# Weight sums made by DMAs that add onto the loaded operand: two of four sums moved, loads six steps ahead

## The chip, the cores and the metric

The kernel runs on one core of a Trainium2 chip. The metric is the device time of one execution in microseconds (us); the time before is the median of three runs. One further execution was taken by the hardware profiler, and every stretch of time below comes from it, counted from the start of its span.

The core has a matrix engine (TensorE, PE in the profile), three engines for elementwise work (VectorE or DVE, ScalarE or ACT, GpSimd or POOL), and a sync engine (SyncE, SP) that issues most transfers. Sixteen DMA engines carry the transfers of all queues. A transfer issued by SyncE goes through the hardware queue (q1 in the profile), one issued by GpSimd through the software queue (q0).

## The reference, cut to what matters

The reference is one layer of a diffusion backbone: a pooling mixer, a layer norm, then a SwiGLU channel mixer and a second layer norm, all in float32.

```
x = layer_norm(ALPHA * x + g1 * pool_mixer(x * (1 + sc1) + sh1), ln_g[0], ln_b[0])
h = x * (1 + sc2) + sh2
gt, up = split(h @ ffn_w_in, 2)          # h 1024 x 1024, ffn_w_in 1024 x 5632
y = (silu(gt) * up) @ ffn_w_out          # 1024 x 2816 times 2816 x 1024
x = layer_norm(ALPHA * x + g2 * y, ln_g[1], ln_b[1])
```

The change touches the second product, `(silu(gt) * up) @ ffn_w_out`.

## The kernel before, in words

Work runs in four stages. The first forms the modulation vectors, the pooling mixer and the first layer norm. The second computes a part of the hidden layer ("gate", matmuls of line 761). The third is a loop of 22 periods over the hidden columns (`period`, matmuls of line 895, about 240 to 530 us). The fourth multiplies the activations by `ffn_w_out` and ends with the second layer norm (matmuls of line 1103, 530 us to the end).

**Seven products instead of eight.** The second product is cut into 2 x 2 blocks: rows of the activations in two halves, columns of `ffn_w_out` in two halves of 512, and the 2816 hidden columns in two sets of 1408 (the index `r`). It is computed by a scheme of Strassen's kind with seven block products. Their left factors are blocks of the activations or sums of them (`a11`, `a2`, `s21`, `s43`), which the loop stores to DRAM. Their right factors are blocks of `ffn_w_out` or sums of them. `PARTS` (line 1050) lists the seven pairs.

**The weight sums.** Four sums of blocks of `ffn_w_out` stand in DRAM as `e_of[0]` to `e_of[3]` (`ed` in the profile). They are made without any compute engine, by DMAs from GpSimd that copy a block to `e_of` or add a block onto what stands there (`accum_op`). `E_STEPS` lists nine such copies and additions, and each is cut into three pieces (`E_PARTS`: 4, 4 and 3 of the 11 column pairs), so there are 27 DMAs of 1 MB or 768 KB. `e_piece(n)` issues one. One is written into each of the loop's periods 1 to 18; the other nine are written into the passes by the last lines of `run_ahead`, one in every third step from step 20 on. GpSimd also computes sums of the input weights in the loop (`all_sums`), each issued before the piece of that period.

**Seven passes, 77 steps.** `sub_pass` carries out one of the seven products as 11 steps of 12 matmuls, over four PSUM banks. A step needs two operands of 128 x 512 (one left, one right), loaded by two DMAs from SyncE into one tile `yraw` (`step_load`, line 1063). Since float32 products are formed from a high and a low part, `step_hi` casts the tile on ScalarE (line 267, out `yhi`) and `step_lo` subtracts on VectorE (line 270, out `ylo`); a step's 12 matmuls are three for each bank: high by high, high by low, low by high.

**What sets the order.** The order is written out by hand: each engine works through its own instructions in the order in which the program issues them, and waits at an instruction until its operands are there. `run_ahead(step)` is called ahead of each step and advances three counters: low parts up to `step + ahead`, high parts one further, loads `LOADS` further. `ahead` grows from `LEAD[0]` to `LEAD[1]` over the first five passes; before the change `LEAD, LOADS = (3, 11), 3`. Loads 0 to 2 are issued in the last but one period of the loop, loads 3 to 6 right after it. Between the steps stand other jobs with a due step of their own: the last activations of the loop and their stores (`last_act`, `a_sums`, `a_more_sums`), loads of the residual rows and their scaling on VectorE, additions of finished banks, and the layer norm's rows in the last two passes (lines 1147 to 1164).

**Buffers.** Tiles of 4 KB per partition lie in 45 places ("big"). In the loop and the passes a new tile takes the place that has been free longest, and its first writer waits until the place's last reader is done.

Of the kernel before, what the change touches and what calls it, by code (L numbers as in the profile page):

```python
# [15 lines left out]
ALU = mybir.AluOpType  # L16
# [8 lines left out]
PAIRS = NF // 2  # L25
# [194 lines left out]
def trunk_kernel(ctx: ExitStack, tc: tile.TileContext, x, c, mod_w, mod_b, ln_g, ln_b, ffn_w_in, ffn_w_out,  # L220
                 pool_w, pool_scale, consts, out):
    nc = tc.nc
# [22 lines left out]
    def done_with(kind, *names):  # L245

        free[kind].extend(taken.pop((kind, name)) for name in names)

    def big(name, dt=F32, shape=(P, 1024)):
        return take("big", name, dt, shape)  # L250
# [269 lines left out]
    def column_half(h):  # L520
        return slice(h * HALF, (h + 1) * HALF)
# [206 lines left out]
    def pieces(name, count):  # L728
        return [dram.tile([P, count, HALF], F32, tag=f"{name}{pair}", name=f"{name}d{pair}", bufs=1)
                for pair in range(NF // 2)]  # L730


    a11_of, a2_of, s21_of, s43_of = pieces("a11", 1), pieces("a2", 2), pieces("s21", 2), pieces("s43", 2)

    e_of = [dram.tile([P, NF // 2, HALF], F32, tag=f"e{n}", name=f"ed{n}", bufs=1) for n in range(1, 5)]
# [163 lines left out]
    def first_product(f, n, w, t):  # L899
        held[f, n] = bank(f"ps_v{f}_{n}")  # L900
        product(held[f, n], weight(f, w), t, True)

    def take_both(f):
        both = tiles["both", f] = half_row(f"both{f}")
        nc.vector.tensor_tensor(both, held.pop((f, 6)), tiles["p1", f // 2][:, f % 2], ALU.add)

    def take_up(f):
        up_b = tiles["up_b", f] = half_row(f"upb{f}")
        nc.vector.tensor_tensor(up_b, held[f, 7], tiles["both", f], ALU.add)
        nc.vector.tensor_tensor(up_b, held[f, 5], up_b, ALU.add)  # L910
# [13 lines left out]
    def act_a(f):  # L924
        a = tiles["a", f]
        nc.vector.tensor_tensor(a[:, 0], held.pop((f, 7)), tiles["both", f], ALU.add)
        nc.vector.tensor_tensor(a[:, 0], a[:, 0], tiles["gate", f // 2][:, f % 2], ALU.mult)

    def a_out(f):

        j, a = f // 2, tiles["a", f]
        if f % 2 == 0:
            nc.sync.dma_start(a11_of[j][:, 0], a[:, 0])
        else:
            nc.sync.dma_start(a2_of[j], a)

    def a_sums(j):

        x, y = tiles["a", 2 * j], tiles["a", 2 * j + 1]
        t = tiles["s21", j] = act_tile(f"s21_{j}")  # L940
        nc.vector.tensor_tensor(t[:, 1], y[:, 1], x[:, 1], ALU.subtract)
        nc.vector.scalar_tensor_tensor(t[:, 0], t[:, 1], -1.0, x[:, 0], ALU.mult, ALU.subtract)
        nc.sync.dma_start(s21_of[j], t)
        done_with("big", f"a_{2 * j}")
# [9 lines left out]
    def a_more_out(j):  # L954
        nc.sync.dma_start(s43_of[j], tiles["s43", j])
        done_with("big", f"s43_{j}")


    def all_sums(f):
        (gate1, up1), (gate2, up2) = ([tiles["raw", f, n][:, q] for q in range(2)] for n in range(2))  # L960
        s = tiles["s", f] = half_row(f"s{f}").rearrange("p (k n) -> p k n", k=4)
        nc.gpsimd.tensor_tensor(s, up1, up2, ALU.add)  # L962
        nc.gpsimd.tensor_tensor(up1, gate1, up1, ALU.subtract)
        nc.gpsimd.tensor_tensor(gate1, s, gate1, ALU.subtract)
        nc.gpsimd.tensor_tensor(gate2, gate2, gate1, ALU.subtract)
# [18 lines left out]
    def split_one(f):  # L984
        one_hi(f), one_lo(f)
        done_with("half", f"s{f}")

    def split_two(f, n):
        two_hi(f, n), two_lo(f, n)
        done_with("big", f"raw{f}_{n}")  # L990
# [36 lines left out]
    first, second = column_half(0), column_half(1)  # L1027
    whole = slice(0, D)
    w_out = ffn_w_out.rearrange("(j r p) d -> p r j d", p=P, r=2)
    res, lines, raw, operands = {}, {}, {}, {}  # L1030

    def block(r, h):

        return w_out[:, r, :, column_half(h)]


    E_STEPS = [(0, block(0, 1), False), (2, block(0, 1), False), (0, block(0, 0), True), (2, block(1, 1), True),
               (1, 0, False), (1, block(1, 1), True), (3, 2, False), (3, block(0, 0), True), (3, block(1, 0), True)]
    IN_LOOP = 18

    E_PARTS = (slice(0, 4), slice(4, 8), slice(8, PAIRS))

    def e_piece(n):

        (dst, src, add), js = E_STEPS[n // 3], E_PARTS[n % 3]
        src = (e_of[src] if isinstance(src, int) else src)[:, js]
        nc.gpsimd.dma_start(e_of[dst][:, js], src, **({"accum_op": ALU.add} if add else {}))
# [4 lines left out]
             (lambda j: s21_of[j][:, 0], lambda j: e_of[1][:, j]),  # L1052
             (lambda j: s21_of[j][:, 1], lambda j: e_of[0][:, j]),
             (lambda j: s43_of[j][:, 0], lambda j: w_out[:, 1, j, second]),
             (lambda j: s43_of[j][:, 1], lambda j: e_of[2][:, j]),
             (lambda j: a2_of[j][:, 1], lambda j: e_of[3][:, j]))
    STEPS = len(PARTS) * PAIRS
    done = {"load": 0, "hi": 0, "lo": 0, "piece": IN_LOOP}

    def step_load(n):  # L1060
        t = raw[n] = big(f"yraw{n}", F32, (P, 2, HALF))
        for m, part in enumerate(PARTS[n // PAIRS]):
            nc.sync.dma_start(t[:, m], part(n % PAIRS))

    def step_hi(n):
        operands[n] = [big(f"yhi{n}", F32R, (P, 2, HALF))]
        take_hi(operands[n][0], raw[n])
# [5 lines left out]

    def advance(kind, upto):
        while done[kind] < min(upto, STEPS):
            {"load": step_load, "hi": step_hi, "lo": step_lo}[kind](done[kind])
            done[kind] += 1

    def run_ahead(step):
        ahead = LEAD[0] + (LEAD[1] - LEAD[0]) * min(step / (5 * PAIRS), 1)  # L1080
        advance("load", int(step + ahead) + LOADS)
        advance("hi", int(step + ahead) + 1)
        advance("lo", int(step + ahead))
        while done["piece"] < 3 * len(E_STEPS) and step >= 20 + 3 * (done["piece"] - IN_LOOP):
            e_piece(done["piece"])
            done["piece"] += 1

    def sub_pass(q, banks, fresh, heads, tails, jobs=()):

# [98 lines left out]
        nc.sync.dma_start(out[i * P : (i + 1) * P, s], res[i][:, s])  # L1188

    HEADS, TAILS = 2, 2  # L1190
    LEAD, LOADS = (3, 11), 3
    u, v, c = {}, {}, {}

    def four(name, after=None):
# [14 lines left out]
    def other_loads(f):  # L1209
        if f + 2 < NF:  # L1210
            weights_load(f + 2)
        if f < NF - 1:
            if f % 2:
                p1_load((f + 1) // 2)
            else:
                silu_load(f // 2)
        n = f - G2_AT
        if n == 0:
            mod_start(G2)
        if 0 <= n < KT:  # L1220
            mod_load(G2, n)

    def g2_steps(f):
        n = f - G2_AT - 1
        if 0 <= n < KT:
            mod_add(G2, n, False)
            done_with("big", f"mw_{G2}_{n}")
        if 0 <= n - KT - 1 < 2:
            g2_half(n - KT - 1)
        if n == KT + 3:  # L1230
            done_with("big", f"acc{G2}")

    def period(f):
        other_loads(f)
        if f % 2 == 0 and f > 3:
            a_more_out(f // 2 - 2)
        if f + 1 < NF:
            all_sums(f + 1)
        if 0 < f <= IN_LOOP:
            e_piece(f - 1)  # L1240
        pair = (f - 3) // 2 if f % 2 and f > 2 else None
        if f > 1:
            act_a(f - 2)
            a_out(f - 2)
            done_with("half", f"both{f - 2}", f"upb{f - 2}")
            done_with("bank", f"ps_v{f - 2}_7")
            if pair is not None:
                done_with("big", f"gate_{pair}")
                a_sums(pair)
        split_two(f, 1)  # L1250
        first_product(f, 5, "s1", t1)
        done_with("big", f"ws1_{f}")
        if f + 1 < NF:
            split_one(f + 1)
            split_two(f + 1, 0)
        g2_steps(f)
        first_product(f, 7, "s3", t3)
        first_product(f, 6, "s2", t2)
        done_with("big", *(f"w0{q}_{f}" for q in "hl"))
        take_both(f)  # L1260
        done_with("bank", f"ps_v{f}_6")
        take_up(f)
        if f % 2:
            done_with("big", f"p1_{f // 2}")
        if f:
            add_s4(f - 1)
            act_b(f - 1)
            done_with("bank", f"ps_v{f - 1}_5")
            add_u2(f - 1)
            done_with("big", *(f"w1{q}_{f - 1}" for q in "hl"))  # L1270
        if pair is not None:
            a_more_sums(pair)

    with tc.manual_schedule():
        for f in range(NF):
            period(f)
            if f == NF - 2:
                advance("load", 3)
                line_load("lg1", ln_g[0]), line_load("lb1", ln_b[0])
        done_with("big", *(name for name in LASTING["big"] if name[:2] in ("t1", "t2", "t3")))  # L1280
        advance("hi", 3)
        advance("lo", 3)
        advance("load", 7)
        f = NF
# [120 lines left out]
```

## Time and profile before

| | before |
|---|---|
| time, median of 3 runs | 761.9 us (760.66, 761.9, 762.62) |
| the profiled execution's own time | 765.08 us |
| its span, first to last instruction | 763.3 us |
| TensorE busy | 730.3 us (96% of the span) |
| VectorE busy | 559.9 us (73%) |
| ScalarE busy | 275.0 us (36%) |
| GpSimd busy | 165.6 us (22%) |
| hardware queue's packets, share of 16 DMA engines | 63.0%, 164.97 MB |
| software queue's packets | 15.4%, 25.95 MB |

Busy time is the union of an engine's instructions; matmuls are pipelined, so a busy TensorE can still run below its best pace, and the number of matmuls in a stretch says more. A DMA share near or above 1 means that the sixteen engines have no room left. In a row that ends in a bracket, the bracket gives the engine's idle time ahead of the instruction and what ended it. DMA rows give the number of issues, the size, and the median time from issue to landing.

### The profile page before, as it was taken

How to read it: one execution, taken by the hardware profiler on the slowest of the kernel's cores; microseconds unless marked ns; L12 is line 12 of the kernel's file. 1: busy time of each engine (PE TensorE's matmuls, PEld its weight loads, DVE VectorE, ACT ScalarE, POOL GpSimd, SP SyncE). 2: the span in 40 equal slices, each digit the busy share in tenths (PEclk: the TensorE clock that was granted, in tenths of full speed). 3: DMA queues.
4: the chain of work that ended last, by engine and by line, in shares of the span. 5: the costliest groups of instructions: out<-in, count | busy, mean ns of one | idle time of the engine just before them, and what ended most of it. 6: DMA issues, size and time to landing. Idle time of an engine off the chain costs nothing.

```text
span 763.3 us, 9102 instructions
## 1 busy us (share of the span) xinstructions
PE 730.3 (96%) x3326; PEld 605.9 (79%) x3326; DVE 559.9 (73%) x675; ACT 275.0 (36%) x353; POOL 165.6 (22%) x126
## 2 busy tenths in 40 slices
PE   6988999999999999999999999999879999999995
PEld 5767988888887888888888888888558888888784
DVE  3598855517198797988889979865369689747985
ACT  0212873435982312213122131123247634344311
POOL 0000000020207554734736447421000000000000
PEclk7578999999999999999999999999999999999998
DMA  8998249685838689999998999699999975764412
GB/s 297 344 409 301 112 148 378 219 247 165 304 113 285 209 276 298 265 278 250 282 297 287 295 202 259 214 288 275 303 365 389 340 234 191 232 229 152 164 58 83
DMA packets 117731, 191.51 MB, mean 251 GB/s; under 512 B 7627, under 2 KB 66707, under 8 KB 117174
## 3 DMA queue, kind: packets, MB, share of 16 engines
q1 hardware_dynamic: 108038, 164.97, 63.0%
q0 software_dynamic: 9648, 25.95, 15.4%
q8 instruction: 26, 0.43, 0.2%
q14 instruction: 19, 0.16, 0.1%
HBM read 150.79 MB, written 66.06 MB: 284 GB/s over the span
## 4 chain that ended last, share of the span: by engine, by line
PE 65%; issue 16%; DMA 11%; DVE 5%; ACT 2%; POOL 0%; SPq 0%; POOLq 0%; DVEq 0%; ACTq 0%
PE ps_v L895 33%; PE ps_gate L761 13%; PE ps_x L1103 7%; DMA yraw<-in_ffn_w_out 4%; PE ps_y L1103 4%; DMA line_lb<-in_ln_b 3%; PE ps_col L506 2%; DVE acc L491 2%; PE ps_pt L461 1%; DMA a11d<-a 1%; PE ps_ox L262 1%; PE ps_ox L264 1%; PE ps_ox L263 1%; DMA x<-in_x 1%; DVE t L270 1%
## 5 line engine op out<-in xcount | busy, mean ns | idle before, releaser
L270 DVE TENSOR_TENSOR ylo<-yraw,yhi 128x1024 fp32r<-128x1024 f32 x77 | 91.8, 1221 | 34.4 <-ACT yhi L267 23.6
L267 ACT CAST yhi<-yraw 128x1024 fp32r<-128x1024 f32 x77 | 80.0, 1052 | 94.4 <-PE ps_x L1103 31.7
L895 PE MATMUL ps_v<-t,w0h 128*128 128x512 f32 x352 | 109.2, 392 | 0.0
L761 PE MATMUL ps_gate<-h,wih 128*128 128x512 f32 x352 | 109.0, 391 | 0.0
L962 POOL TENSOR_TENSOR s<-raw,raw 128x512 f32<-128x512 f32 x22 | 33.1, 1504 | 320.4 <-DMA raw<-in_ffn_w_in 312.0
L918 ACT ACTIVATE a<-a 128x512 f32<-128x512 f32 x22 | 13.9, 632 | 230.0 <-DVE a L917 230.0
L895 PEld LDWEIGHTS ps_v<-t,w0h 128*128 128x128 f32 x352 | 66.1, 188 | 14.5 <-issue 1.0
L761 PEld LDWEIGHTS ps_gate<-h,wih 128*128 128x128 f32 x352 | 65.7, 188 | 13.8 <-issue 0.5
L1103 PE MATMUL ps_x<-yhi 128*128 128x512 f32 x176 | 69.6, 395 | 5.1 <-ACT u L1310 2.7
L1103 PE MATMUL ps_x<-ylo,yhi 128*128 128x512 f32 x176 | 69.8, 397 | 3.3 <-DVE ylo L270 3.3
L491 DVE SCALAR_TENSOR_TENSOR acc<-mw,s_col,acc 128x1024 f32<-128x1024 f32 x42 | 54.9, 1307 | 23.1 <-DMA mw<-in_mod_w 22.5
L895 PE MATMUL ps_v<-t,w0l 128*128 128x512 f32 x176 | 68.6, 390 | 1.5 <-DVE w0l L270 1.5
L1103 PE MATMUL ps_x<-yhi,ylo 128*128 128x512 f32 x176 | 69.2, 393 | 0.0
L761 PE MATMUL ps_gate<-h,wil 128*128 128x512 f32 x176 | 68.5, 389 | 0.0
L895 PE MATMUL ps_v<-t,ws 128*128 128x512 f32 x264 | 63.4, 389 | 0.0
L895 PEld LDWEIGHTS ps_v<-t,ws 128*128 128x128 f32 x264 | 49.5, 188 | 10.3
L895 PE MATMUL ps_v<-t,w1h 128*128 128x512 f32 x176 | 54.1, 389 | 0.0
L895 PE MATMUL ps_v<-h,w1h 128*128 128x512 f32 x176 | 54.1, 389 | 0.0
L1103 PE MATMUL ps_y<-yhi 128*128 128x512 f32 x132 | 51.4, 390 | 0.9 <-DVE yv L1348 0.9
L1103 PE MATMUL ps_y<-ylo,yhi 128*128 128x512 f32 x132 | 51.4, 389 | 0.0
L1103 PE MATMUL ps_y<-yhi,ylo 128*128 128x512 f32 x132 | 51.3, 389 | 0.0
L1125 POOL TENSOR_TENSOR yrow<-yrow,line_lg 128x224 f32<-128x224 f32 x1 | 0.9, 913 | 229.3 <-ACT yrow L1185 229.3
(156 smaller groups left out, 1409.5 us busy)
## 6 DMA issues: line engine op xcount, KB each, us to landing
mw<-in_mod_w SPq DMA_DIRECT2D x48, 512.0 KB, 9.7
raw<-in_ffn_w_in SPq DMA_DIRECT2D x88, 256.0 KB, 6.7
ed<-in_ffn_w_out POOLq DMA_DIRECT2D x14, 1024.0 KB, 11.1
wi<-in_ffn_w_in SPq DMA_DIRECT2D x22, 512.0 KB, 6.2
yraw<-ed SPq DMA_DIRECT2D x44, 256.0 KB, 4.6
yraw<-in_ffn_w_out SPq DMA_DIRECT2D x33, 256.0 KB, 6.0
pd<-pk SPq DMA_DIRECT2D x11, 512.0 KB, 5.4
gd<-gk SPq DMA_DIRECT2D x11, 512.0 KB, 2.9
```

The lines of the kernel that those rows point to most:

```text
L262: nc.tensor.matmul(ps, lh, rh, start=first, stop=False)
L263: nc.tensor.matmul(ps, lh, rl, start=False, stop=False)
L264: nc.tensor.matmul(ps, ll, rh, start=False, stop=last)
L267: nc.scalar.copy(hi, src)
L270: nc.vector.tensor_tensor(lo, src, hi.bitcast(F32), ALU.subtract)
L491: nc.vector.scalar_tensor_tensor(acc, w, s_col[:, k : k + 1], acc, ALU.mult, ALU.add)
L506: nc.tensor.matmul(tiles["ps_col", j][:, n * WIDE : (n + 1) * WIDE], t[:, n * P : (n + 1) * P], by, start=first and n == 0, stop=last and ...
L761: nc.tensor.matmul(ps, x, y, start=k == n == 0, stop=k % 4 == 3 and n == 2, skip_group_check=k > 3)
L895: nc.tensor.matmul(ps, x, y, start=fresh and first, stop=last, skip_group_check=not fresh)
L918: nc.scalar.activation(a[:, 1], a[:, 1], ACT.Silu)
L962: nc.gpsimd.tensor_tensor(s, up1, up2, ALU.add)
L1103: nc.tensor.matmul(ps, s[x][:, r * P : (r + 1) * P], t[y][:, d], start=fresh and j == m == 0, stop=j == PAIRS - 1 and m == 2, skip_group_c ...
```

## The change

Two of the four weight sums are no longer made in DRAM. `E_STEPS` keeps four steps, hence twelve pieces, which make `e_of[0]` and `e_of[1]`; all twelve are issued in the loop, in the periods of `E_TIMES` (1, 2, 4, 5, 7, 8, 10, 11, 13, 14, 16, 17), and none in the passes. In the sixth and seventh products, parts 5 and 6, the right operand is loaded as one summand (a block of `ffn_w_out`, or `e_of[1]`), and a DMA from GpSimd then adds the other summand, a block of `ffn_w_out`, onto the loaded half tile on the chip: 22 DMAs of 256 KB (`step_sum`). A fourth counter, "sum", stands two steps behind the loads. `LEAD, LOADS` goes from `(3, 11), 3` to `(3, 9), 6`: loads are issued six steps ahead of the low part instead of three, and the low part is made at most 9 steps ahead of its matmuls instead of 11.

```diff
-    E_STEPS = [(0, block(0, 1), False), (2, block(0, 1), False), (0, block(0, 0), True), (2, block(1, 1), True),
-               (1, 0, False), (1, block(1, 1), True), (3, 2, False), (3, block(0, 0), True), (3, block(1, 0), True)]
-    IN_LOOP = 18
+    E_STEPS = [(0, block(0, 1), False), (0, block(0, 0), True), (1, 0, False), (1, block(1, 1), True)]
+    E_TIMES = [1 + 3 * n // 2 for n in range(len(E_STEPS) * len(E_PARTS))]
...
-             (lambda j: s43_of[j][:, 1], lambda j: e_of[2][:, j]),
-             (lambda j: a2_of[j][:, 1], lambda j: e_of[3][:, j]))
+             (lambda j: s43_of[j][:, 1], lambda j: w_out[:, 0, j, second]),
+             (lambda j: a2_of[j][:, 1], lambda j: e_of[1][:, j]))
+
+    ADDED = {5: lambda j: w_out[:, 1, j, second], 6: lambda j: w_out[:, 1, j, first]}
...
+    def step_sum(n):
+        if n // PAIRS in ADDED:
+            nc.gpsimd.dma_start(raw[n][:, 1], ADDED[n // PAIRS](n % PAIRS), accum_op=ALU.add)
...
         advance("load", int(step + ahead) + LOADS)
+        advance("sum", int(step + ahead) + LOADS - 2)
         advance("hi", int(step + ahead) + 1)
         advance("lo", int(step + ahead))
-        while done["piece"] < 3 * len(E_STEPS) and step >= 20 + 3 * (done["piece"] - IN_LOOP):
-            e_piece(done["piece"])
-            done["piece"] += 1
...
-    LEAD, LOADS = (3, 11), 3
+    LEAD, LOADS = (3, 9), 6
...
-        if 0 < f <= IN_LOOP:
-            e_piece(f - 1)
+        if f in E_TIMES:
+            e_piece(E_TIMES.index(f))
```

More of the change, by code (lines that the diff above doesn't have):

```diff
@@ L1054, in trunk_kernel @@
              (lambda j: s43_of[j][:, 0], lambda j: w_out[:, 1, j, second]),
-             (lambda j: s43_of[j][:, 1], lambda j: e_of[2][:, j]),
-             (lambda j: a2_of[j][:, 1], lambda j: e_of[3][:, j]))
+             (lambda j: s43_of[j][:, 1], lambda j: w_out[:, 0, j, second]),
+             (lambda j: a2_of[j][:, 1], lambda j: e_of[1][:, j]))
+    ADDED = {5: lambda j: w_out[:, 1, j, second], 6: lambda j: w_out[:, 1, j, first]}
     STEPS = len(PARTS) * PAIRS
-    done = {"load": 0, "hi": 0, "lo": 0, "piece": IN_LOOP}
+    done = {"load": 0, "sum": 0, "hi": 0, "lo": 0}
     def step_load(n):
@@ L1075, in advance @@
         while done[kind] < min(upto, STEPS):
-            {"load": step_load, "hi": step_hi, "lo": step_lo}[kind](done[kind])
+            {"load": step_load, "sum": step_sum, "hi": step_hi, "lo": step_lo}[kind](done[kind])
             done[kind] += 1
@@ L1280, in trunk_kernel @@
         done_with("big", *(name for name in LASTING["big"] if name[:2] in ("t1", "t2", "t3")))
+        advance("sum", 3)
         advance("hi", 3)
```

## The prediction

> **What bounds the kernel now.** I read the page first, then busy times by stage, then what TensorE waited for in the one stage that stands out, and then who held the DMA engines there.
>
> Totals of the page:
>
> ```profile
> span 763.3 us, 9102 instructions
> PE 730.3 (96%) x3326; PEld 605.9 (79%) x3326; DVE 559.9 (73%) x675; ACT 275.0 (36%) x353; POOL 165.6 (22%) x126
> ```
>
> TensorE (PE) is busy 96% of the span, so only places where it does not run at its pace can give anything. Busy time by stretch, one row for the loop over the hidden columns, then one for the first two of the seven output passes together, one for the third and one for the sixth (the columns: busy us and instructions of PE, weight loads, DVE, ACT, POOL, then granted clock, DMA share, GB/s):
>
> ```profile
> 240.00:530.00 290.00, 289.56 (x1273) 239.03 (x1274) 246.15 (x265) 62.91 (x82) 144.82 (x104) 1.00 0.93 267
> ```
>
> ```profile
> 530.27:603.27 73.00, 64.53 (x266) 50.42 (x265) 45.66 (x45) 36.99 (x39) 0.00 (x0) 0.98 1.04 354
> 603.27:633.19 29.92, 29.92 (x134) 24.77 (x133) 25.58 (x30) 11.49 (x11) 0.00 (x0) 1.00 0.69 233
> ...
> 693.05:723.00 29.95, 29.90 (x132) 24.41 (x131) 26.22 (x38) 15.96 (x22) 0.00 (x0) 1.00 0.47 158
> ```
>
> The loop leaves TensorE idle 0.44 us in 290, so nothing is to be had there. A pass of 132 products takes 29.92 us when undisturbed (2.72 us for each of its 11 steps), but the first two take 73.00 instead of 59.84: **13.16 us are lost between 530 and 603**, and the DMA share there is 1.04. What TensorE waited for in that stretch, and then in the rest:
>
> ```profile
> PE ps_x L1103 <- DVE ylo L270: 3.3, 5, 0.8
> PE ps_x L1103 <- ACT u L1310: 2.7, 1, 2.7
> PE ps_x L1103 <- ACT yhi L267: 2.3, 2, 2.0
> ```
>
> ```profile
> PE ps_y L1103 <- DVE yv L1348: 0.9, 1, 0.9
> ```
>
> These named waits (8.3 us of the 13.16; the rest lies between and in the products around them, where the granted clock is 0.98 on average against 1.00 after) are all on the two halves of a split operand and on a copy behind them on ScalarE. The split itself waits for its load:
>
> ```profile
> 537.58 1.05 ACT L267 CAST yhi<-yraw 128x1024 fp32r<-128x1024 f32 x1 [4.01 <-DMA yraw<-in_ffn_w_out]
> ```
>
> ```profile
> 538.65 1.23 DVE L270 TENSOR_TENSOR ylo<-yraw,yhi 128x1024 fp32r<-128x1024 f32 x1 [6.26 <-ACT yhi L267]
> 539.80 0.69 DVE L926 TENSOR_TENSOR a<-ps_v,both 128x512 f32<-128x512 f32 x1
> 540.52 0.69 DVE L927 TENSOR_TENSOR a<-a,gate 128x512 f32<-128x512 f32 x1
> ```
>
> The loads are late because the DMA engines are shared. DMA queues and landings, first from 489 to 550, then from 580 to 640:
>
> ```profile
> q0 software_dynamic: 3344, 8.65, 65.5%
> q1 hardware_dynamic: 3432, 8.41, 39.0%
> ...
> yraw<-a11d SPq DMA_DIRECT2D x9, 256.0 KB, 17.8
> ...
> yraw<-in_ffn_w_out SPq DMA_DIRECT2D x8, 256.0 KB, 19.2
> ```
>
> ```profile
> q1 hardware_dynamic: 8792, 17.05, 80.1%
> ...
> yraw<-ed SPq DMA_DIRECT2D x20, 256.0 KB, 5.4
> ```
>
> From 489 to 550 the software queue takes 65.5% of the sixteen engines (40 us of 61) and an operand's load needs 17.8 to 19.2 us to land; without that queue 5.4 us do, although the engines are 80% busy. The software traffic is the weight sums' last nine pieces. The code writes them into the passes from step 20 on (line 1084), some 55 us after the first pass starts, but they wait for nothing on their engine, so POOL issues them as soon as the loop's sums are done:
>
> ```profile
> 489.19 1.65 POOL L1047 DMA_DIRECT2D ed<-ed  x3
> ...
> 527.90 1.23 POOL L1047 DMA_DIRECT2D ed<-in_ffn_w_out  x1 [5.94 <-DMA ed<-in_ffn_w_out]
> ```
>
> They are in flight just when the first loads of the passes must land.
>
> The Trainium skill (DMA: Bandwidth & Descriptors, section Queues, rings and completion order) says that a DMA engine takes turns between the queues that have work, packet by packet. By that rule a queue of its own does not protect the loads from POOL's pieces, and the trace agrees: with both queues loaded the landing is some 18 us against 5.4.
>
> **The change, part by part.** *The nine pieces leave the handover.* Fifteen of 27 pieces go; the twelve that stay are issued in periods 1 to 17 of the loop, under TensorE's 289.56 busy us, as 18 were before. The 40 us of engine time from 489 to 550 fall away entirely. What is left there, 39.0% of 61 us or 23.8 us, fits more than twice. A load should land in about 5.4 us, so steps 3 to 6, issued from 515.35 to 533 before (order below), land before they are due at 530.27 + 3 × 2.72 = 538.4. The first stall is then gone, and with it the chain behind it, because DVE's last activations (540.52) were late only behind the waiting ylo. The copy of the banks (2.7 us) waited behind the same late casts. Gain: up to 13.16 us. The fewer pieces in the loop give nothing; if its cover were gone, its raw loads would land earlier, which is no loss either.
>
> *Loads six steps ahead of the low half instead of three.* At the first step loads 7 to 9 are issued at once, ahead of the last stores. Before, SyncE's order there was
>
> ```profile
> 515.35 0.32 SPq L1063 DMA_DIRECT2D yraw<-a11d  x1
> ...
> 535.38 0.32 SPq L955 DMA_DIRECT2D s43d<-s  x1
> ...
> 543.82 0.32 SPq L1063 DMA_DIRECT2D yraw<-a11d  x1
> ```
>
> with loads 3 to 6 ahead of the store at 535.38 and load 7 at 543.82. In the new order loads 7 to 9 stand only behind that store and the store of the 21st column's activation, so they go out about 531 to 534 and land by about 540; they are due at 549.3. Load 10 reads a block that the kernel itself has just stored, so SyncE stands until that store lands; behind it stand the residual rows and the loads from 11 on, due from 560. In buffers, three more raw tiles against two steps less of split halves make 27 in use late in the passes against 28 (two halves per step of lead, plus raws, plus the step at work), so no new wait for space. Cost 0.
>
> *22 sums by DMA on the loaded operand.* The trace shows no such DMA onto the chip's memory. Issue costs POOL 1.23 us (row above), and POOL has nothing else to do after 530. Three pieces issued in 1.65 us show that it does not wait for a landing. The landing of the pieces:
>
> ```profile
> DMA to landing us min/median/max: 5.9/10.4/23.8
> ```
>
> For 256 KB I take 6 us. The load is issued 15 steps ahead, the cast stands 10 ahead: 13.6 us for load 5.4, issue 1.2, sum 5.9 to 10.4, that is 12.5 to 17.0. A cast is late by 0 to 3.4 us, and queued behind it on ScalarE are only later casts and the row squares; the low half has 9 steps, 24.5 us, before TensorE wants it. Cost on the path 0. By the Trainium skill's fit for a software DMA (DMA: Bandwidth & Descriptors, Anatomy of one DMA), a sum would land in an estimated 2.6 us; the pieces above, four times as large, give no sign of so little, and the sum of terms is the same.
>
> *Engine time of the sums.* Bounds for a packet: 87.5 ns (580 to 640: 80.1% of 60 us × 16 over 8792) and 191 ns (489 to 550: 65.5% of 61 × 16 over 3344). One sum is 128 rows of 2 KB, so 0.70 to 1.53 us of sixteen engines, 15 to 34 us for 22. I take 1.53, the row of the adding queue. The stretch that gets them:
>
> ```profile
> 645.00:708.00 63.00, 63.00 (x279) 52.16 (x279) 42.35 (x57) 28.89 (x35) 0.00 (x0) 1.00 0.63 208
> ```
>
> It has 39.7 us of engine time, with the sums 55 to 73 us of 63: full, and at the upper end 10 us behind by its end, which the 24.5 us of lead hide. Without that cover it would cost up to 10 us.
>
> *Lead 9 instead of 11.* Two splits (hi 1.05 us, lo 1.23 us) move from the sixth pass to behind the banks' additions at the start of the last one:
>
> ```profile
> 723.01 2.48 DVE L1348 TENSOR_TENSOR yv<-ps_y,yv 128x512 f32<-128x512 f32 x4
> 725.40 0.69 DVE L1200 TENSOR_TENSOR yv<-yv,g 128x512 f32<-128x512 f32 x1
> 726.00 1.28 DVE L1160 SCALAR_TENSOR_TENSOR yrow<-yrow,mw,line_lg 128x1024 f32<-128x1024 f32 x1
> ```
>
> ```profile
> 746.58 0.69 DVE L1200 TENSOR_TENSOR c<-ps_y,g 128x512 f32<-128x512 f32 x1 [1.11 <-PE ps_y L1103]
> ...
> 754.06 0.69 DVE L1200 TENSOR_TENSOR c<-ps_y,g 128x512 f32<-128x512 f32 x1 [1.50 <-PE ps_y L1103]
> ```
>
> TensorE needs the first of these low halves 9 × 3 products or 6.1 us into the last pass, at about 729.9, and the second 0.7 us later. By DVE's order they come at 725.5 + 1.2 = 726.7 behind the four additions, and, behind a scaling (0.69), a row's centring (1.28) and an addition to a row (0.69), at 726.7 + 2.7 + 1.2 = 730.6: the second is just in time. DVE's idle time further on, 1.11 and 1.50 us, takes up the 2.5 us that they cost there. The price on the path is between 0 and 2.5; I take 0.5.
>
> **Sum.** −13.16 + 0.5 = −12.7 us on the profiled execution, whose own time is 765.08 us (1.8 us more than its span): 752.4. The median of the runs shown, 761.9, is 3.2 us below that execution, so **749.2 us**.
>
> **Rivals.** *B, half stays.* The start of the passes is limited by one order on SyncE, with its stores, and by DVE's last activations, not by the engines' load: for it, load 7 stood behind four other DMAs; against, these were slow on full engines and DVE waited for casts. Half of 13.16 left: 755.8.
> *C, the sums disturb DVE.* In the sixth pass DVE is busy 26.22 of 29.95 us and TensorE already waits 0.9 us for it; casts late by 3.4 us hold up low halves and the additions in order behind them. 749.2 + 3.4 = 752.6. Against: lead.
> *D, slower: the adding DMAs become the bound of the last three passes.* With y us of engine time per step, TensorE stalls 22 × (y − 2.72) − 24.5 us. It decides from y = 3.83; the whole gain is gone at 4.41, and at 4.6 the stall is 16.9: 766.1 us. For it, the full engines of 489 to 550 and landings up to 23.8; against, y by the rows is 0.63 × 2.72 + 0.70 to 1.53 = 2.4 to 3.2.
> *E, the change does not relieve the handover*, because the deeper prefetch fills the engines itself (share 1.04 over 530 to 603 though from 580 on there is no software traffic): about 762. Against: nothing late is left to catch up.
>
> **Numbers.** Forecast 0.68, B 0.13, C 0.09, E 0.05, D 0.05. A measurement of this kernel tells about 0.3% (2.3 us) from no change. Faster: forecast, B, C, 0.90; same: E; slower: D. The forecast's own range is 747.5 to 751.5 (cost of the last pass 0 to 2.5, runs ± 1); taking in C and B, the range is 747.3 to 756.5.
>
> **What would show it.** In the changed profile no software traffic between 489 and 640; operand loads from 500 to 535 landing in 4 to 8 us; the first two passes in about 60 us with no wait on ylo, yhi or u; 22 software DMAs of 256 KB between about 640 and 710; DMA share there 0.9 to 1.05, and still 29.9 us per pass. I am wrong if the first two passes still take over 64 us (B, E), if a pass from the fifth on takes over 31 us with ScalarE waiting for the software queue (C, D), or if the last pass begins with a wait on a low half.

## The result, and the profile after

The changed kernel takes 748.88 us (median of 4 runs, 747.78 to 749.97) against 761.28 us of the kernel before beside it (4 runs, 760.64 to 762.62). The ratio is 0.9836, with a 95% interval of 0.9806 to 0.9866: 12.4 us less, where 12.7 were forecast. The profiled execution takes 749.97 us with a span of 748.2 us. Line numbers move by three in the last stage: the passes' matmuls of line 1103 now stand in 1106.

Busy time of the changed kernel by stretch: the loop, the first two passes together, and the third (columns as before):

```profile
240.00:527.60 287.60, 287.60 (x1266) 237.41 (x1265) 238.75 (x261) 62.92 (x82) 126.72 (x87) 1.00 0.78 234
527.70:587.55 59.85, 59.85 (x266) 49.56 (x265) 43.91 (x44) 34.92 (x37) 0.00 (x0) 1.00 0.99 364
587.55:617.47 29.92, 29.92 (x134) 24.77 (x133) 25.46 (x30) 11.30 (x11) 0.00 (x0) 1.00 0.62 211
```

The first two passes take 59.84 us, twice 29.92, instead of 73.00: the stretch has no loss left. What TensorE waited for from 500 us to the end:

```profile
PE ps_y L1106 <- DVE yv L1352: 0.9, 1, 0.9
```

The waits on `ylo`, `yhi` and `u` are gone; the 0.9 us at the last pass, which stood there before too, is the only one left. DMA queues and landings, from 489 to 550, and then from 640 to 720 where the new sums run:

```profile
q1 hardware_dynamic: 6374, 14.58, 67.1%
...
yraw<-in_ffn_w_out SPq DMA_DIRECT2D x18, 256.0 KB, 5.4
yraw<-a11d SPq DMA_DIRECT2D x11, 256.0 KB, 4.2
```

```profile
q1 hardware_dynamic: 6361, 12.62, 44.8%
q0 software_dynamic: 3168, 5.77, 40.5%
...
yraw<-in_ffn_w_out POOLq DMA_DIRECT2D x22, 256.0 KB, 7.1
yraw<-a2d SPq DMA_DIRECT2D x11, 256.0 KB, 7.4
```

No software traffic is left from 489 to 550, and an operand's load lands in 4.2 to 5.9 us instead of 17.8 to 19.2. In the late stretch the sums bring the software queue back, with 40.5% of the engines, and loads there need 6.9 to 7.8 us, against 3.1 to 5.1 us in the kernel before.

The two profiled spans differ by 15.1 us, more than the medians. The first matmul of the loop stands at 227.4 in the one and at 225.0 in the other (matmuls of the loop: times in ns, then first and last start, of the kernel before and of the changed one):

```profile
L895 PE MATMUL ps_v<-t,ws x264: 388/389/389, 227.4 to 513.7; 128*128 128x512 f32 x132
```

```profile
L895 PE MATMUL ps_v<-t,ws x264: 388/389/389, 225.0 to 511.1; 128*128 128x512 f32 x132
```

Nothing that the change edits runs before the loop. In the fourteen kernels profiled for this study that start lies anywhere from 223.3 to 227.4 us, so the 2.4 us are the spread of the front stages and no effect of the change.

### The profile page after: what moved, and what is told of

The parts are those of the page before. It is cut to its first block, busy times and chain, and to the rows that moved or that the text cites. A ratio compares the mean times of both kernels' runs of the same rounds, so it can differ in the third digit from the quotient of the medians.

```text
span 748.2 us, 9131 instructions
## 1 busy us (share of the span) xinstructions
PE 723.9 (97%) x3326; PEld 604.8 (81%) x3326; DVE 554.9 (74%) x675; ACT 274.1 (37%) x353; POOL 168.3 (22%) x133
## 4 chain that ended last, share of the span: by engine, by line
PE 84%; DVE 7%; DMA 3%; ACT 3%; issue 2%; POOL 0%; SPq 0%; POOLq 0%; DVEq 0%; ACTq 0%
PE ps_v L895 39%; PE ps_x L1106 16%; PE ps_gate L761 14%; PE ps_y L1106 8%; PE ps_col L506 2%; DVE acc L491 2%; DVE ylo L270 1%; PE ps_ox L262 1%; PE ps_ox L263 1%; PE ps_ox L264 1%; DMA x<-in_x 1%; DMA consts<-in_consts 1%; ACT h L699 1%; DMA mw<-in_mod_w 1%; DVE t L270 1%
## 5 line engine op out<-in xcount | busy, mean ns | idle before, releaser
L267 ACT CAST yhi<-yraw 128x1024 fp32r<-128x1024 f32 x77 | 78.4, 1051 | 81.7 <-DMA yraw<-in_ffn_w_out 23.4
L962 POOL TENSOR_TENSOR s<-raw,raw 128x512 f32<-128x512 f32 x22 | 31.5, 1432 | 319.3 <-DMA raw<-in_ffn_w_in 300.5
L1068 POOL DMA_DIRECT2D yraw<-in_ffn_w_out x22 | 18.7, 853 | 195.6 <-PE ps_x L1106 163.6
```

Source lines behind the costliest of these rows:

```text
L267: nc.scalar.copy(hi, src)
L1068: nc.gpsimd.dma_start(raw[n][:, 1], ADDED[n // PAIRS](n % PAIRS), accum_op=ALU.add)
```

## The experiments

Each ran beside the kernel before on its chip, whose median there was 760.7 to 764.6 us. "First two passes" and "sixth and seventh pass" are measured from the first matmul to the first of the next pass (to the last matmul's end for the seventh).

| kernel | median us | ratio, 95% interval | first two passes | sixth and seventh pass |
|---|---|---|---|---|
| before | 761.28 | | 72.8 | 61.2 |
| changed | 748.88 | 0.9836 (0.9806 to 0.9866) | 59.8 | 61.2 |
| before, no late pieces | 750.72 | 0.9855 (0.9816 to 0.9893) | 60.3 | 61.1 |
| before, deep loads only | 762.11 | 1.0000 (0.9975 to 1.0024) | 71.6 | 61.2 |
| changed, late pieces back | 762.19 | 1.0002 (0.9982 to 1.0023) | 71.2 | 61.2 |
| before, pieces held | 749.20 | 0.9836 (0.9791 to 0.9880) | 59.8 | 61.2 |
| before, all pieces in the loop | 750.76 | 0.9862 (0.9820 to 0.9903) | 60.0 | 61.2 |
| changed, (3, 11), 3 | 762.05 | 1.0003 (0.9983 to 1.0024) | 60.1 | 72.8 |
| changed, (3, 9), 3 | 763.52 | 0.9987 (0.9965 to 1.0008) | 61.8 | 71.2 |
| changed, (3, 9), 4 | 751.29 | 0.9863 (0.9826 to 0.9899) | 59.8 | 61.2 |
| changed, (3, 11), 5 | 757.01 | 0.9895 (0.9863 to 0.9928) | 59.8 | 68.4 |
| changed, (3, 8), 8 | 753.31 | 0.9895 (0.9861 to 0.9929) | 59.8 | 65.6 |
| changed, sums on both halves | 773.29 | 1.0133 (1.0089 to 1.0178) | 59.8 | 84.3 |
| changed, every sum twice | 834.00 | 1.0949 (1.0906 to 1.0993) | 59.8 | 143.7 |

### Is it the late pieces, or the depth of the loads?

**The kernel before without the nine late pieces.**

```diff
-               (1, 0, False), (1, block(1, 1), True), (3, 2, False), (3, block(0, 0), True), (3, block(1, 0), True)]
+               (1, 0, False), (1, block(1, 1), True)]
...
-             (lambda j: a2_of[j][:, 1], lambda j: e_of[3][:, j]))
+             (lambda j: a2_of[j][:, 1], lambda j: e_of[2][:, j]))
```

> The kernel before without the nine late pieces (the fourth weight sum is not made; the last product reads the third sum instead, so its values differ). Theory (the nine pieces collide with the first loads of the passes, and that is the whole loss): the first two passes together take 59.8 to 60.5 us and the time is 748.5 to 750.5 us. Rival (loads that are issued too late are the cause, whatever else the engines carry): the first two passes stay above 68 us and the time is 757 us or more.

Measured: 750.72 us, first two passes 60.27 us. The old depth of the loads, the old lead and the 18 pieces in the loop stand; taking the nine pieces away is enough for the gain. The median is 0.2 us above the range; the passes are where the theory put them.

**The kernel before with the new depth and lead only.**

```diff
-    LEAD, LOADS = (3, 11), 3
+    LEAD, LOADS = (3, 9), 6
```

> The kernel before with LEAD, LOADS = (3, 9), 6 and nothing else. Theory (collision): loads 7 to 9 go out earlier but still land in about 18 us between the late pieces, and steps 3 to 6 are not helped: first two passes 68 us or more, time 756 to 761.5 us. Rival (depth of the loads): first two passes under 62 us, time 749 to 751 us.

Measured: 762.11 us, ratio 1.0000. Its queues from 489 to 550:

```profile
q0 software_dynamic: 3277, 8.10, 62.5%
q1 hardware_dynamic: 4229, 9.82, 44.7%
...
yraw<-a11d SPq DMA_DIRECT2D x11, 256.0 KB, 13.7
yraw<-in_ffn_w_out SPq DMA_DIRECT2D x11, 256.0 KB, 16.5
```

Five more load DMAs are issued in the stretch and they land somewhat earlier, but the first two passes still need 71.65 us. The time is 0.6 us above the range's upper end, and the rival's 749 to 751 is refuted.

**The changed kernel with nine late pieces put back**, into `run_ahead` as they stood:

```diff
         advance("lo", int(step + ahead))
+        while late["n"] < 3 * len(LATE) and step >= 20 + 3 * late["n"]:
+            late_piece(late["n"])
+            late["n"] += 1
+
+    LATE = [(3, e_of[1], False), (3, block(0, 0), True), (3, block(1, 0), True)]
...
```

> The changed kernel with nine pieces put back into the passes as the kernel before writes them (from step 20 on, nothing holds them, their result is not used). Theory: loads from 489 to 550 land in about 18 us again, the first two passes take 68 to 73 us and the time is 756 to 762 us. Rival (depth of the loads): first two passes under 62 us, time 749 to 751 us.

Measured: 762.19 us, 0.2 us above the range, ratio 1.0002, first two passes 71.18 us. Its queues from 489 to 550:

```profile
q0 software_dynamic: 3155, 7.23, 58.4%
q1 hardware_dynamic: 4564, 10.87, 49.2%
...
yraw<-in_ffn_w_out SPq DMA_DIRECT2D x12, 256.0 KB, 16.2
```

The loads of `a11d` land in 13.4 us there, not in the 18 expected. With the pieces the loss is back, although everything else of the change stands: without the pieces there is none, and with them it is there at either depth of the loads.

### Is it their amount or their place?

**The kernel before with the late pieces held until their step:**

```diff
+            held_back(int(step))
             e_piece(done["piece"])
             done["piece"] += 1
+    def held_back(step):
+        t = small(f"hold{step}", (P, 1), 1, "hold")
+        nc.gpsimd.tensor_copy(t, operands[max(operands)][0][:, 0, :1].bitcast(F32))
```

> The kernel before; each of the nine late pieces first waits, through a copy of one column on GpSimd, for the newest cast operand of its step, so that it starts near the step at which the code writes it, from about 585 us on, instead of at 489. Theory: the first loads land in about 5 us, the first two passes take 60 to 62 us, the pieces spread over the third and fourth pass at a share below 1; time 749 to 752 us with all four sums still made in DRAM. Rival (it is the amount of software traffic, wherever it runs, or the depth of the loads): 757 us or more.

Measured: 749.20 us, first two passes 59.84 us. GpSimd in that kernel around its first held piece and its last:

```profile
572.18 6.61 POOL L1091 COPY hold<-yhi 128x1 f32<-128x1 f32 x1 [84.86 <-ACT yhi L267]
578.73 0.60 POOL L1047 DMA_DIRECT2D ed<-ed  x1
...
646.01 0.18 POOL L1091 COPY hold<-yhi 128x1 f32<-128x1 f32 x1 [10.90 <-ACT yhi L267]
646.45 1.23 POOL L1047 DMA_DIRECT2D ed<-in_ffn_w_out  x1 [0.26 <-issue]
```

All 27 pieces are made in DRAM, as before the change, and the time equals that of the changed kernel. They start at 579 to 646 instead of 489 to 528, when the first two passes are nearly over. The engines are full there too: from 579 to 650 the two queues take 106.8% of them and an operand's load lands in 6.7 to 10.6 us. Yet TensorE never stops, as its row for the end of that stretch shows:

```profile
620.00:650.00 30.00, 30.00 (x134) 24.82 (x133) 24.99 (x27) 10.26 (x11) 5.65 (x6) 1.00 1.09 302
```

So the total of the traffic is not what costs, nor full engines as such. The pieces cost where they meet the first loads of the passes. There the low halves are made three steps ahead; by `run_ahead` it is some six to nine steps while the held pieces run. The run spreads them out as well (47.9% of the engines against 65.5%), and how much of the relief comes from the later place and how much from the thinner stream it does not separate.

**The kernel before with all 27 pieces in periods 1 to 18 of the loop:**

```diff
-    done = {"load": 0, "hi": 0, "lo": 0, "piece": IN_LOOP}
+    done = {"load": 0, "hi": 0, "lo": 0, "piece": 3 * len(E_STEPS)}
...
         if 0 < f <= IN_LOOP:
-            e_piece(f - 1)
+            for n in range(3 * (f - 1) // 2, 3 * f // 2):
+                e_piece(n)
```

> The kernel before with all 27 pieces in periods 1 to 18 of the loop, three in every two periods. Theory: first two passes 59.8 to 60.5 us; the loop's engines carry 0.93 of 290 us already, with 40 us more they are full (about 1.05), so that the loop loses 0 to 8 us to late loads of input weights; time 749 to 757 us. Rival (the loop hides every transfer): loop unchanged, 749 us. Rival (depth of the loads): 757 us or more.

Measured: 750.76 us, first two passes 59.97 us. The loop in that kernel:

```profile
240.00:528.00 288.00, 288.00 (x1268) 237.82 (x1267) 233.45 (x262) 64.39 (x82) 137.50 (x102) 1.00 0.99 284
```

The time lies in the theory's range too; the loop's row decides, and the rival that the loop hides every transfer was right: the loop hides every piece, at a share of 0.99 instead of 0.93, without a wait of TensorE. What costs 13 us at the start of the passes costs nothing in the loop.

### What the new depth is for

**The changed kernel with LEAD, LOADS = (3, 11), 3.**

> The changed kernel with LEAD, LOADS = (3, 11), 3, so that the sum stands one step ahead of the cast and three behind nothing else. Theory: the first two passes need no deeper loads, 59.8 to 60.5 us; in the last passes a load, an issue and a sum take some 14 us and the cast is late, but 11 steps (30 us) of lead cover that: 748 to 750 us, the same as the changed kernel. Rival (the six steps are needed): first two passes above 64 us, or TensorE waits on low halves in the last three passes, 752 us or more.

Measured: 762.05 us, the whole gain lost, but in another place. The first two passes take 60.1 us, as expected; the sixth and seventh take 72.8 us instead of 61.2. My expectation was wrong there: the lead did not cover the late casts. TensorE's wait in that stretch:

```profile
PE ps_y L1106 <- DVE yv L1352: 10.2, 1, 10.2
```

It does not wait for an operand. It waits for VectorE to add up the sixth product's banks, onto which the seventh product then accumulates.

**The changed kernel with (3, 9), 3, and with (3, 11), 5.**

> The changed kernel with LEAD, LOADS = (3, 9), 3: only the depth of the loads is undone. Theory P (a raw tile lives from its load to its low half; with the sum in that path this is some 15 us, so three in flight allow a step every 5 us): the loads slip behind TensorE, VectorE works through late low halves ahead of the banks' additions, and the last two passes take 65 to 72 us instead of 61.2: time 753 to 760 us. Rival Q (the shorter lead, 9 instead of 11, is what the changed kernel needs, since the additions then stand behind two low halves less): last two passes under 62.5 us, 749 to 750.5 us.

> The changed kernel with LEAD, LOADS = (3, 11), 5: the old lead with deeper loads. Theory P: five raw tiles in flight allow a step every 3 us, close to TensorE's 2.72; the last two passes take 61 to 64 us and the time is 749 to 752.5 us. Rival Q (lead 11 puts the additions behind two late low halves more): last two passes above 66 us, 754 us or more.

Measured: 763.52 us with 71.2 us for the last two passes, and 757.01 us with 68.4 us. Both depth and lead matter: lead 9 alone doesn't help, against rival Q, and five tiles in flight with lead 11 still lose 7.2 us, against theory P's 61 to 64 us. Each account's figure for the two passes came out in the run in which the other's failed. The 763.52 us lie above P's 753 to 760, in part because the first two passes lose 2.0 us as well (61.8 us). From this I formed theory R, that the chain from a load's issue to its low half must fit into LOADS steps whatever the lead, and tried it with a fourth depth.

> The changed kernel with LEAD, LOADS = (3, 9), 4. Theory R, formed after the runs with 3 and 5: VectorE adds the sixth product's banks in order behind the low half that is 9 or 11 steps ahead, so a chain from a load's issue to its low half has to fit into LOADS steps of 2.72 us, whatever the lead. The chain is some 17.6 us (load 7.4, issue 0.85, sum 7.1, cast 1.05, low half 1.2): with 4 steps, 10.9 us, the last two passes lose 5 to 8.5 us against the changed kernel's 61.2: time 754 to 758 us. Rival P (three tiles in flight set a pace, four allow 15 / 4 = 3.75 us per step): the loss grows over all 22 steps, 12 us or more, 760 us.

Measured: 751.29 us, and the last two passes take 61.2 us: no loss at all, where R asked for 5 to 8.5 us. Theory R falls with the others. What the six kernels do show is where the time goes. VectorE in the sixth pass, from about TensorE's first matmul to the first addition of a bank, in the kernel before, the changed one, and then with (3, 9), 4, with (3, 9), 3, with (3, 11), 5 and with (3, 11), 3:

```profile
693.05:723.01 29.96, 29.90 (x132) 24.41 (x131) 26.23 (x39) 15.96 (x22) 0.00 (x0) 1.00 0.47 158
```

```profile
677.30:707.40 30.10, 30.04 (x133) 24.55 (x131) 26.22 (x38) 17.90 (x24) 6.79 (x8) 1.00 0.89 234
```

```profile
680.30:710.40 30.10, 30.09 (x133) 24.59 (x131) 26.18 (x38) 17.11 (x23) 7.64 (x9) 1.00 0.98 258
```

```profile
680.60:718.70 38.10, 30.11 (x133) 24.59 (x131) 29.19 (x42) 19.21 (x25) 8.78 (x11) 0.93 0.90 227
```

```profile
676.90:711.70 34.80, 30.05 (x133) 24.56 (x131) 29.20 (x43) 19.32 (x25) 7.64 (x9) 0.99 0.84 220
```

```profile
676.90:716.30 39.40, 30.08 (x133) 24.59 (x131) 30.51 (x43) 20.48 (x26) 7.64 (x9) 0.94 0.85 208
```

And the low halves among that work, then the additions of the fifth pass's banks (busy us, mean ns, idle ahead), in the changed kernel, with (3, 9), 3 and with (3, 11), 5:

```profile
L270 DVE TENSOR_TENSOR ylo<-yraw,yhi 128x1024 fp32r<-128x1024 f32 x11 | 13.3, 1217 | 3.6 <-ACT yhi L267 3.6
...
L1338 DVE TENSOR_TENSOR c<-ps_x,u 128x512 f32<-128x512 f32 x1 | 0.7, 692 | 0.7 <-PE ps_x L1106 0.7
```

```profile
L270 DVE TENSOR_TENSOR ylo<-yraw,yhi 128x1024 fp32r<-128x1024 f32 x12 | 14.5, 1218 | 11.0 <-ACT yhi L267 11.0
...
L1338 DVE TENSOR_TENSOR c<-ps_x,u 128x512 f32<-128x512 f32 x4 | 2.5, 680 | 0.0
```

```profile
L270 DVE TENSOR_TENSOR ylo<-yraw,yhi 128x1024 fp32r<-128x1024 f32 x12 | 14.5, 1219 | 6.2 <-ACT yhi L267 6.2
...
L1338 DVE TENSOR_TENSOR c<-ps_x,u 128x512 f32<-128x512 f32 x4 | 2.5, 682 | 0.0
```

In the three kernels without a loss, the kernel before among them, VectorE is busy 26.2 us and idle 3.6 us on casts, so that its pass is full already. In the slow three it is busy 29.2 to 30.5 us: it enters the sixth pass behind, with three more of the fifth pass's additions and a low half or two more to do, and it is idle 6.2 to 11.0 us on casts. Work and waits fill 35 to 39 us, and the sixth pass's additions stand at their end. So a late sum costs through VectorE's order and not through a missing operand. Why four tiles in flight suffice with lead 9 and five do not with lead 11 is not settled: the additions stand behind the low half two steps further on, and the loads there land in 9.9 us against 6.1 (below), but no run separates the two.

```profile
yraw<-in_ffn_w_out SPq DMA_DIRECT2D x10, 256.0 KB, 6.1
```

```profile
yraw<-in_ffn_w_out SPq DMA_DIRECT2D x8, 256.0 KB, 9.9
```

**The changed kernel with (3, 8), 8.**

> The changed kernel with LEAD, LOADS = (3, 8), 8: two steps more of depth, one less of lead. Theory R: the chain fits already into six steps, so eight give nothing more; first two passes 59.8 us, last two 61 to 61.5 us, 748 to 750 us. Rival (the changed kernel still loses something in the sums' path): the wait of 0.9 us at the last pass goes, 747 to 748 us. If the shorter lead is too short, TensorE waits on low halves: 751 us or more.

Measured: 753.31 us. The sixth pass is as in the changed kernel, but the seventh takes 34.7 us instead of 30.2:

```profile
PE ps_y L1106 <- DVE ylo L270: 2.6, 1, 2.6
PE ps_y L1106 <- DVE yv L1352: 0.9, 1, 0.9
```

One step less of lead leaves one more low half behind the additions at the start of the last pass, and there it is late. The third of the cases written down came true: lead 8 is too short. With lead 9, in the changed kernel, the second and last low half behind the additions ends at 714.56, an estimated 0.5 us before TensorE needs it (30 matmuls of 0.227 us after the first of the last pass, at 708.23).

### What the sums cost, and what covers them

**Every sum issued twice** (the second summand is added twice, in `step_sum`):

```diff
-            nc.gpsimd.dma_start(raw[n][:, 1], ADDED[n // PAIRS](n % PAIRS), accum_op=ALU.add)
+            for _ in range(2):
+                nc.gpsimd.dma_start(raw[n][:, 1], ADDED[n // PAIRS](n % PAIRS), accum_op=ALU.add)
```

> The changed kernel with each of the 22 sums issued twice (the second summand is added twice, so the values differ): 44 software DMAs. It tests the price and the cover of the sums. Theory, with 164 ns per packet as the changed kernel shows (1.31 us of engine time per sum): a step asks 1.7 + 2.6 = 4.3 us of the engines in 2.72, TensorE waits 22 x 1.6 - 24.5 = 11 us in the last three passes: 758 to 762 us. Rival (a single sum costs the engines half of that, as a plain load does): 2.0 x 1.4 + 1.7 = 3.1 us per step, hidden: 749 to 750 us.

Measured: 834.00 us, far above both. The edit brought a wait of its own that I had not put down: the second sum adds onto bytes that the first one writes, so GpSimd stands until the first has landed, with the next tile's sum behind it:

```profile
645.95 1.81 POOL L1069 DMA_DIRECT2D yraw<-in_ffn_w_out  x2 [4.99 <-DMA yraw<-in_ffn_w_out]
654.46 1.71 POOL L1069 DMA_DIRECT2D yraw<-in_ffn_w_out  x2 [6.70 <-DMA yraw<-s43d]
664.27 1.72 POOL L1069 DMA_DIRECT2D yraw<-in_ffn_w_out  x2 [8.10 <-DMA yraw<-ed]
```

That is a pair of sums every 5.5 to 10.7 us over the 22 steps, where a step of TensorE takes 2.72. It says nothing on the engines' time, so the same amount was tried without that wait.

**The sum added onto both halves of the tile** (`step_sum` issues it for m = 0 and m = 1, onto `raw[n][:, m]`; the products' values differ):

> The changed kernel with 44 sums of 256 KB: the same summand is added onto the right half and also onto the left half of each of the 22 tiles (so the values differ). Twice the engine time of the sums without one sum waiting for another. Theory (a packet's 164 ns are engine time): 4.3 us of engine time in a step of 2.72 us, the loads and sums fall behind by some 35 us over 22 steps, and with 24.5 us of lead TensorE loses 8 to 15 us: 757 to 764 us. Rival (most of a packet's time is waiting, in which the engine serves the other queue): under 752 us.

Measured: 773.29 us, slower than the kernel before. Queues from 640 to 720, and TensorE's wait:

```profile
q0 software_dynamic: 5588, 10.20, 69.7%
q1 hardware_dynamic: 5751, 10.59, 39.9%
```

```profile
PE ps_y L1107 <- ACT yhi L267: 22.5, 1, 22.5
```

The queues' shares add up to 109.6% of the engines: they are full, the software packets do cost engine time, and the rival (hidden, under 752 us) is refuted. The direction is the theory's, the size is not: TensorE lost 23.1 us in the last two passes where 8 to 15 were expected.

The wait is put down to a cast, but the cast that ends just then (begun at 727.43) is that of a step nine steps further on than the matmul that waits. What came free at that moment is the first bank. VectorE adds it at 727.68, in order behind a low half that had waited for its cast:

```profile
725.34 1.23 DVE L270 TENSOR_TENSOR ylo<-yraw,yhi 128x1024 fp32r<-128x1024 f32 x1 [2.47 <-ACT yhi L267]
...
727.68 2.48 DVE L1353 TENSOR_TENSOR yv<-ps_y,yv 128x512 f32<-128x512 f32 x4
```

So this is VectorE's order again. From 651 to 719 the casts come about every 4.0 us, so that a step's loads and two sums take the full engines 4.0 us, where the expectation had 4.3. By its sum, 22 × (4.0 − 2.72) = 28 us, some 5 us were covered and not 24.5; that is an estimate.

## Why the prediction was right, point by point

**The bound and its cause.** Right, and shown. The 13.16 us lay in the first two passes, the nine late pieces on the software queue caused them, and they came from GpSimd running ahead of the step at which the code writes them. Removing, restoring and holding the pieces moved the loss each time. The Trainium skill (DMA: Bandwidth & Descriptors, Queues, rings and completion order) says that an engine takes turns between queues with work; the landings of 13 to 19 us with both queues loaded and 4 to 6 us with one agree. They do not prove the rule: with both queues at work but the engines at 0.86, from 640 to 720 in the changed kernel, loads land in 6.9 to 7.8 us, so how full the engines are counts as well.

**−13.16 + 0.5.** The first term measured −13.0 (72.8 to 59.8 between the first matmuls of the passes; the row in the prediction ended 0.2 us later). The second measured 0: the last pass takes 30.18 us against 30.20, and the last row's scaling on VectorE starts 0.43 us after the start of the last matmul in both kernels. VectorE's idle time took up the two low halves, as the working said; ahead of that scaling it stood at 1.50 us and is now:

```profile
738.47 0.69 DVE L1203 TENSOR_TENSOR c<-ps_y,g 128x512 f32<-128x512 f32 x1 [0.45 <-PE ps_y L1106]
```

From the last matmul's end to the span's end it is 9.25 us before and 9.76 after, but that half microsecond is not this term: the kernel before with the new depth and lead only has the same idle time of 0.45 us and 8.83 us to the end. What makes it is not known.

**Fewer pieces in the loop give nothing.** Right; the loop's matmuls take the same time at a share of 0.78 as at 0.93, and at 0.99.

**The deeper loads, cost 0.** Right as a price, but incomplete. I looked at them as a part of the start of the passes, where they do little: 60.1 us (lead 11) and 61.8 us (lead 9) with the old depth, 59.8 with the new. That depth also sets what the sums cost I saw only as a cast late by 0 to 3.4 us, which the lead would hide; with the old depth the changed kernel is no faster than the one before. That the chosen depth was enough was in part luck. Loads 7 to 9 went out together where the working put them, right behind the store of the 21st column:

```profile
527.80 0.32 SPq L933 DMA_DIRECT2D a11d<-a  x1
528.22 0.38 SPq L1064 DMA_DIRECT2D yraw<-a11d  x1
...
530.79 0.41 SPq L1064 DMA_DIRECT2D yraw<-in_ffn_w_out  x1
```

**The sums' price.** The landing of 7.1 us lies in 5.9 to 10.4, where I took 6; the issue took 0.84 to 0.90 us against 1.23. The 22 sums took 40.5% of the sixteen engines' 80 us, so a sum is 1.47 us of engine time where I took 1.53. (A packet took 164 ns, between the bounds of 87.5 and 191, but a sum has 144 packets, 3168 over 22, and not the 128 of its rows; the 1.31 us of an expectation above counts 128.) The engines were at 0.86 from 640 to 720, where the working had them full. By the Trainium skill's fit (DMA: Bandwidth & Descriptors, Anatomy of one DMA) a sum would land in an estimated 2.6 us; measured were 7.1 beside the loads, so on busy engines the trace's own landings were the better price.

**The cover of 24.5 us.** This step was wrong, though it didn't reach the sum. I set the sums' lateness against the nine steps of lead before TensorE. The runs show another limit that comes first: VectorE is full in the sixth pass, with 26.2 us of work and 3.6 us of waits for casts, and low halves that come late push the additions of the banks back. Rival C named this mechanism and its place; I gave it 3.4 us and a chance of 0.09, but with the old depth it costs 10 to 11.6 us. The depth of the change keeps it at zero. Rival D's formula used the same cover and put its point of decision too late: at the 4.0 us per step that the sums on both halves showed it gives 3.7 us of stall, and TensorE lost 23.1.

**Rivals B and E** are refuted by the 59.84 us: neither SyncE's order nor the prefetch's own traffic held anything back.

## What to carry to other kernels

An engine that works ahead of the others carries its DMAs with it: where the code writes an issue says little about when it goes out, so look at its time in the trace, and give it something to wait for if it must come later. Here that alone (749.20 us) was worth as much as making the sums on the chip (748.88). And a lead counted in steps before the consumer is no cover if a third engine has other work in order behind the late instruction; count what that engine has to do and to wait for in the stage instead.

## What the runs showed of the hardware

After some of its stalls TensorE ran at half its pace for a time. In the kernel before it waited 2.04 and 0.76 us shortly before 557.8, and the granted clock, the third figure from the end of these rows, fell to 0.50 and came back:

```profile
558.00:560.00 2.00, 2.00 (x5) 1.59 (x6) 1.80 (x3) 1.63 (x2) 0.00 (x0) 0.50 1.04 397
...
562.00:564.00 2.00, 2.00 (x10) 1.67 (x9) 1.75 (x2) 0.00 (x0) 0.00 (x0) 1.00 0.82 231
```

From 557.8 to 561.3 the matmuls start 0.43 us apart instead of 0.227, which makes 1.7 us of the 13.0 lost. With (3, 9), 3 the pace is halved for 4.4 us behind a wait of 8.8. A wait of 2.6 us with (3, 8), 8 is followed by it too, but the wait of 2.7 us at 573 in the kernel before is not (1.00 from 570 to 580), and what decides no run here shows.

The waits that the trace names sum to 8.3 us. Most of the other 3 us lies in the same pauses: a named wait counts from the end of the matmul ahead of it, which the profile puts 0.39 to 0.50 us behind its start, while undisturbed matmuls start every 0.227 us.
